# Paired first loads, first products by parts, and a LayerNorm whose sums go through fp32r products

## The chip, the cores and the metric

The kernel runs on one NeuronCore of a Trainium2 chip. A NeuronCore has five engines that run side by side, each through its own queue, in order: TensorE (PE) multiplies matrices, VectorE (DVE) works on two tensors or a tensor and a number, ScalarE (ACT) applies functions and casts, GpSimd (POOL) does simple tensor work and issues some transfers, SyncE (SP) issues most transfers. They wait for one another through semaphores. The metric is the time of one execution on the device in microseconds; less is better.

## What is computed

One layer of a decoder trunk, for 256 new positions of a prompt and 8 x 4 sampled ones, together T = 288 columns. All is float32 at the boundary.

```python
h = rmsnorm(x, norm1_g)                                    # 2048 wide
a, gate, z = split(h @ w_in + b_in, 3)                     # 1024 each
u = a * sigmoid(gate)
c = silu(layernorm(depthwise_causal_conv(u, conv_w, conv_b), ln_g, ln_b))
d = multiscale_pool(z)                                     # windows 2, 4, 8, 16
p = (d @ pool_w per group) * pool_scale
x = x + concat(c, p) @ w_out
x = x + square(relu(rmsnorm(x, norm2_g) @ w_ff1)) @ w_ff2  # 8192 wide inside
y = rmsnorm(x, norm_f)
```

The outputs are y for both groups of requests and the new states of the convolution and of the pool. The LayerNorm takes mean and variance over the 1024 channels of the convolution:

```python
mu = mean(xf); var = mean(square(xf - mu))
y = (xf - mu) * rsqrt(var + EPS) * g + b
```

## The kernel before

The activations lie transposed: channels on the 128 partitions, the 288 columns along the row. A weight block is 128x1024 (four rows of tiles of 256 columns); a product multiplies a 128x128 tile of it with 128x288 of activations into a bank of PSUM. Since the matrix unit takes fp32r, a rounded float32, for its fast products, each float is split in two, a high part (the cast) and a low part (what is left). Each 128x128x288 step is then three products: high by high, high by low and low by high. `wr` is a raw block of weights as it is loaded, `whi` its high part (cast on ACT, line 275), `wlo` its low part (a subtraction on DVE, line 280, or on POOL in halves, line 283, or a transfer that adds). Numbers behind such a name count the blocks. High and low parts have five buffers each: `whi73` goes where `whi67` was, one stage of loads earlier by the rotation, and waits until the last product that reads `whi67` has been made. All such products are made by `mm` on line 306, from `gemm`, which goes through a list of (row k, bank m, part of the weight, part of the activation).

The order of the stages is fixed by `SEQUENCE`: the input projection, by pairs of banks (c0 to c7 for the convolution, p0 to p3 for the pool), the small products of the pool groups (P0 to P3), w_out in eight pairs of banks (`ac18` to `ac21` and so on) first over the pool's half (`dx`, whose parts are made on line 510) and then over the convolution's (`mx`, line 592), then the two feed-forward products, which make up the larger part of the time. A scheduler places the instructions of each engine by a priority, which is the order in which the code is written; `later()` adds to it, so that what stands under it is put behind other ready work.

The start is special, since nothing is loaded. `first_weights` loads the rows of the first four banks, `first_x` the activations, in the order of `FIRST`: the first two rows apart, then pairs. The very first weights and the second ones are issued on ACT's queue, with a table load between them; all else on SP's. `first_split` makes high and low parts, x before weights. The first four banks are multiplied row by row (`singly=True`). The RMSNorm is applied after the products: `squares` adds the squares of x, `rsqrt_sums` (lines 242 to 257) sums them on PE in 96x3, takes the root on ACT and corrects it on DVE, and `spread` brings the 288 values to all partitions by three products with `ident`. They go into the stream of products by the table `between`.

The LayerNorm of the convolution works the same way inside the w_out stage. `ln_mean` (two fp32 products, each two passes on PE, into `pmean`) stands in the pair g = 5; `ln_sums` subtracts the mean from the four tiles c1 to c4 (line 559), squares and adds them (`q`), and sums by `rsqrt_sums` in g = 6; `ln_rows` spreads them in g = 7. Then each tile is multiplied by the row (`n`, line 587), goes through Silu twice, once for each half (line 590), and is split (`mx`, lines 592 and 593).

ACT has one table of functions loaded at a time; `load_table` runs a tiny activation (`few`, line 209) in order to load another. `inverse_root` (lines 232 to 237) is the other form of the corrected root, for a whole tile of 288 columns; it is used before the feed-forward.

Of the kernel before, what the change touches and what calls it, by code (L numbers as in the profile page):

```python
# [86 lines left out]
def trunk_kernel(ctx: ExitStack, tc: tile.TileContext, io):  # L87
# [97 lines left out]
    def first_weights(k, n, queue):  # L185
        if k % 2 == 0:
            raws.append(by_pair(raw_tile()))
        src = io["w"][1 + k // 8 : 4 + k // 8 : 2].rearrange("b p k c -> p b k c")
        queue.dma_start(raws[k // 2][:, :, k % 2 : k % 2 + n, :], src[:, :, k % 8 : k % 8 + n, :])

    def first_x(k, n):
        nc.sync.dma_start(xT[:, k : k + n, :], io["xT"][:, k : k + n, :])

    FIRST = [(0, 1), (1, 1)] + [(k, 2) for k in range(2, KT, 2)]
    first_weights(0, 1, nc.scalar)
    nc.sync.dma_start(vec[:, 0:NG], io["vec"][:, 0:NG])
    for k, n in FIRST[:6]:
        first_x(k, n)
        if k > 1:
            first_weights(k, n, nc.sync)  # L200
# [10 lines left out]
    with tc.issue_after(load_table(AF.Sqrt, ones[:, 0:1]).ins):  # L211
        first_weights(1, 1, nc.scalar)
# [14 lines left out]
    cst = const.tile([P, 32], F32, name="cst")  # L227
# [83 lines left out]
    def gemm(banks, rhs, m_outer=False, between={}, classes="", singly=False):  # L311
# [4 lines left out]
        units = [(k, 2) for k in range(0, n, 2)]  # L316
        if singly:
            units = [(k, 1) for k in range(n)]
        pairs = [(k, width, m) for k, width in units for m in range(len(banks))]
        if m_outer:  # L320
            pairs.sort(key=lambda p: p[2])
        parts = {1: ((0, 0, 0), (0, 0, 1), (0, 1, 0)), 2: ((0, 0, 0), (1, 0, 0), (0, 1, 0), (1, 1, 0), (1, 0, 1), (0, 0, 1))}
        todo, begins = [], {}
        for k, width, m in pairs:
            if m == 0:
                begins[len(todo)] = k
            todo += [(k + d, m, w, x) for d, w, x in parts[width]]
# [27 lines left out]
    def first_split(k0, n):  # L355
        for k in range(k0, k0 + n):
            if k % 2 == 0:
                hx.extend(halves(act2("hx")))
            hh, hl = hx[k]
            if k == 0:  # L360
                nc.vector.tensor_scalar(hh, xT[:, k, :], v("norm1_g", k), None, op0=ALU.mult)  # L361
            else:
                nc.scalar.activation(hh, xT[:, k, :], AF.Copy, scale=v("norm1_g", k))
# [70 lines left out]
    def conv_pair(i, banks):  # L434
# [7 lines left out]
        if i == N8 - 1:  # L442
            load_table(AF.Sqrt, tg[:, 0:1])
# [335 lines left out]
```

## Time and profile before

| | |
|---|---|
| median of 3 runs | 1085.36 us (1085.34 to 1086.2) |
| the profiled execution | 1084.97 us, span 1082.9 us |
| TensorE busy | 1071.1 us, 99%, 8198 records |
| VectorE busy | 636.5 us, 59% |
| ScalarE busy | 477.4 us, 44% |
| GpSimd busy | 173.8 us, 16% |
| first product of the layer | 5.58 us |
| first product that reads mx | 219.33 us |

The profiled execution is one of its own; a sum worked out on its trace is compared with its own time. A record of PE is one pass: an fp32 product makes two. Products overlap in the pipeline, so a record's length (about 0.29 us for 288 columns) is more than the distance between two starts (0.13 us). A row of the timeline gives the start, the length to the end of the last of the joined instructions, the engine, the line, the operation, output and inputs, how many were joined, and in brackets the idle time before and what ended it. Rows of groups by line have the least, median and longest length in ns and the first and last start.

### The profile page before, as it was taken

The numbers are of one execution on the slowest core, as the hardware profiler recorded it, in microseconds if no ns is written. First come the engines' busy times: TensorE is split into PE (matmuls) and PEld (weight loads), VectorE is DVE, ScalarE is ACT, GpSimd is POOL, SyncE is SP. The second block draws the span as 40 slices with busy tenths as digits, with TensorE's granted clock in tenths as the row PEclk, the third lists the DMA queues.
The fourth block names the chain that finished last, engine by engine and source line by source line (L and its number), as shares of the span: only waits on it lengthen the run. The fifth ranks groups of instructions, "written<-read, shape, count | busy, mean of one in ns | idle before, by whom it ended". The sixth has DMA issues, their size and how long they took to land.

```text
span 1082.9 us, 19574 instructions
## 1 busy us (share of the span) xinstructions
PE 1071.1 (99%) x8198; PEld 1068.5 (99%) x8198; DVE 636.5 (59%) x817; ACT 477.4 (44%) x584; POOL 173.8 (16%) x180
## 2 busy tenths in 40 slices
PE   9999999999999999999999999999999999999996
PEld 8999999999999999999999999999999999999996
DVE  8899999678655544445544444545544445554552
ACT  8654455475544433334443333444433334444441
POOL 0878979512000000000000000000000000000001
PEclk9999999999999999999999999999999999999998
DMA  9896477545555555555555555555555555555522
GB/s 333 281 268 182 137 209 231 172 152 176 173 163 170 174 168 165 175 164 168 175 169 165 174 167 167 174 171 164 172 169 166 173 172 164 171 172 163 172 78 88
DMA packets 58696, 190.71 MB, mean 176 GB/s; under 512 B 6256, under 2 KB 12016, under 8 KB 58608
## 3 DMA queue, kind: packets, MB, share of 16 engines
q1 hardware_dynamic: 56336, 184.09, 53.0%
q0 software_dynamic: 1008, 3.67, 1.8%
q10 hardware_dynamic: 1264, 1.70, 0.5%
q8 instruction: 64, 1.05, 0.4%
q14 instruction: 24, 0.20, 0.1%
HBM read 185.16 MB, written 4.28 MB: 175 GB/s over the span
## 4 chain that ended last, share of the span: by engine, by line
PE 76%; issue 21%; ACT 1%; DMA 1%; DVE 1%; POOL 0%; SPq 0%; POOLq 0%; DVEq 0%
PE ac L306 75%; DMA wr<-in_w 1%; PE pp L306 0%; ACT whi L275 0%; DVE wlo L280 0%; POOL xT L715 0%; ACT n L590 0%; DVE z_all L414 0%; ACT L209 0%; ACT z_all L412 0%; PE pt L306 0%; PE pmean L306 0%; POOLq L765 0%; DVE xT L690 0%; DVE n L587 0%
## 5 line engine op out<-in xcount | busy, mean ns | idle before, releaser
L275 ACT CAST whi<-wr 128x1024 fp32r<-128x1024 f32 (+1 forms) x341 | 355.5, 1043 | 557.5 <-PE ac L306 536.0
L280 DVE TENSOR_TENSOR wlo<-wr,whi 128x1024 fp32r<-128x1024 f32 (+1 forms) x297 | 363.7, 1225 | 348.4 <-ACT whi L275 348.4
L306 PE MATMUL ac<-ax,whi 128*128 128x288 f32 x2048 | 351.1, 292 | 0.0
L306 PE MATMUL ac<-fx,whi 128*128 128x288 f32 x2048 | 350.2, 292 | 0.0
L306 PEld LDWEIGHTS ac<-ax,whi 128*128 128x128 f32 x2048 | 296.0, 187 | 0.0
L306 PEld LDWEIGHTS ac<-fx,whi 128*128 128x128 f32 x2048 | 295.7, 187 | 0.0
L306 PE MATMUL ac<-ax,wlo 128*128 128x288 f32 x1024 | 217.4, 292 | 0.0
L306 PE MATMUL ac<-fx,wlo 128*128 128x288 f32 x1024 | 216.4, 292 | 0.0
L306 PEld LDWEIGHTS ac<-ax,wlo 128*128 128x128 f32 x1024 | 162.6, 187 | 0.0
L306 PEld LDWEIGHTS ac<-fx,wlo 128*128 128x128 f32 x1024 | 162.3, 187 | 0.0
L306 PE MATMUL ac<-hx,whi 128*128 128x288 f32 x768 | 136.2, 293 | 0.7 <-DVE hx L361 0.3
L715 POOL TENSOR_TENSOR xT<-xT,rf 128x288 f32<-128x288 f32 x4 | 3.0, 792 | 800.1 <-ACT rf L719 800.1
L306 PEld LDWEIGHTS ac<-hx,whi 128*128 128x128 f32 x768 | 113.3, 188 | 1.4 <-ACT whi L275 0.9
L283 POOL TENSOR_TENSOR wlo<-wr,whi 128x512 fp32r<-128x512 f32 x74 | 100.6, 1415 | 35.4 <-ACT whi L275 34.4
L457 DVE SCALAR_TENSOR_TENSOR pc<-u_all,vec,pc 128x256 f32<-128x256 f32 x232 | 99.5, 483 | 1.9 <-ACT pc L454 0.7
L306 PE MATMUL ac<-hx,wlo 128*128 128x288 f32 x384 | 86.2, 293 | 0.3 <-DVE wlo L280 0.2
L306 PEld LDWEIGHTS ac<-hx,wlo 128*128 128x128 f32 x384 | 62.7, 188 | 0.7 <-DVE wlo L280 0.7
L306 PE MATMUL ac<-dx,whi 128*128 128x288 f32 x256 | 46.1, 296 | 0.3 <-ACT dx L510 0.3
L306 PE MATMUL ac<-mx,whi 128*128 128x288 f32 x256 | 45.2, 294 | 0.1
L659 DVE SCALAR_TENSOR_TENSOR t<-ac,r 128x576 f32<-128x576 f32 x32 | 24.2, 758 | 25.2 <-PE ac L306 25.2
L306 PEld LDWEIGHTS ac<-dx,whi 128*128 128x128 f32 x256 | 37.9, 188 | 0.7 <-ACT dx L510 0.6
L306 PEld LDWEIGHTS ac<-mx,whi 128*128 128x128 f32 x256 | 37.5, 188 | 0.6 <-ACT mx L592 0.3
(130 smaller groups left out, 515.0 us busy)
## 6 DMA issues: line engine op xcount, KB each, us to landing
wr<-in_w SPq DMA_DIRECT2D x335, 512.0 KB, 3.7
wlo<-in_w POOLq DMA_DIRECT2D x7, 512.0 KB, 8.5
xT<-in_xT SPq DMA_DIRECT2D x7, 288.0 KB, 7.1
out_u_out<-u_all SPq DMA_DIRECT2D x1, 1208.0 KB, 8.9
u_all<-in_hist_c SPq DMA_DIRECT2D x8, 136.0 KB, 5.6
wr<-in_w SPq DMA_DIRECT2D x4, 256.0 KB, 3.5
out_z_out<-z_all SPq DMA_DIRECT2D x1, 668.0 KB, 8.9
z_all<-in_hist_p SPq DMA_DIRECT2D x4, 152.0 KB, 7.7
```

What stands on the lines that cost most here:

```text
L275: nc.scalar.copy(hi, raw)
L280: nc.vector.tensor_tensor(lo, raw, f32(hi), op=ALU.subtract)
L283: nc.gpsimd.tensor_tensor(lo[:, j : j + 2, :], raw[:, j : j + 2, :], f32(hi[:, j : j + 2, :]), op=ALU.subtract)
L306: last = nc.tensor.matmul(*args, **kw)
L457: nc.vector.scalar_tensor_tensor(out=dst, in0=up[:, w : w + SEQ], scalar=cwv[:, w : w + 1], in1=pc, op0=ALU.mult, op1=ALU.add)
L659: nc.vector.scalar_tensor_tensor(out=t, in0=bk[:, :, :T], scalar=0.0, in1=both(rows2[0]), op0=ALU.max, op1=ALU.mult)
L715: eng.tensor_tensor(xk, xk, r[:, None, :].to_broadcast([P, n, T]), op=ALU.mult)
```

## The change

Six things are changed together.

1. *First loads.* x and weights are loaded in pairs of rows throughout. The first weights come as two transfers, one for each block of two banks, with both rows of the pair; the first on ACT's queue, the second on SP's behind the joint x of rows 0 and 1. ACT's queue issues one transfer at the start, not two.
2. *First split.* The high cast of a weight comes ahead of the x parts, and the low part of a weight ahead of the low parts of x. The first two pairs are cast in two halves, by blocks of banks.
3. *First products.* For the first four banks, `by_part` lists all high by high products of a pair of rows, then all with the low weights, then all with the low x; the first pair does so for two banks and then for the other two. The table `classes`, which sets the alternation of two kinds of products, now covers the start.
4. *Table load.* The table with Sqrt is loaded after the last `dx` of the pool and not after the last sigmoid.
5. *LayerNorm.* The two inputs of the mean are split into fp32r parts (`hm`: two casts on ACT, a subtraction on POOL and one on DVE), and the mean is four fp32r products with `means_c`, a copy of `ones` (1/1024 everywhere) in fp32r, made by POOL at the start. The sum of squares is split likewise (`hs`), two fp32r products bring the sums to all partitions at once (`pt`), so that `spread` is not needed; the root is taken of the whole 128x288, and `inverse_root` corrects it (reciprocal and three steps on 128x288 in place of 96x3).
6. *Priority.* From the subtraction of the mean to the split of `mx`, all stands under `later(-LATER)`, that is ahead of other work.

```diff
-    def first_weights(k, n, queue):
...
+    def first_weights(k, queue, blocks):
         src = io["w"][1 + k // 8 : 4 + k // 8 : 2].rearrange("b p k c -> p b k c")
+        queue.dma_start(raws[k // 2][:, blocks], src[:, blocks, k % 8 : k % 8 + 2, :])
+
+    def first_load(k):
+        raws.append(by_pair(raw_tile()))
+        nc.sync.dma_start(xT[:, k : k + 2, :], io["xT"][:, k : k + 2, :])
+        if k:
+            first_weights(k, nc.sync, slice(0, 2))
+        else:
+            first_weights(k, nc.scalar, slice(0, 1))
+            first_weights(k, nc.sync, slice(1, 2))
...
-    with tc.issue_after(load_table(AF.Sqrt, ones[:, 0:1]).ins):
-        first_weights(1, 1, nc.scalar)
+    load_table(AF.Sqrt, ones[:, 0:1])
...
+        if by_part:
+            for k in range(0, n, 2):
+                sets = [range(len(banks))] if k else [range(2), range(2, len(banks))]
+                for last, ms_ in enumerate(sets, 1 - len(sets)):
+                    for part, (w, x) in enumerate(((0, 0), (1, 0), (0, 1))):
...
+                        todo += [(k + (1 - d if x else d), m, w, x) for m in ms_ for d in range(2)]
...
-        if i == N8 - 1:
-            load_table(AF.Sqrt, tg[:, 0:1])
...
-    chain.append(gemm(pair0 + pair1, hx, between={15: first_sums}, singly=True))
-    third = conv_products(2, between={2: first_rows}, classes="01" * 18 + TURN)
+    chain.append(gemm(pair0 + pair1, hx, between={15: first_sums}, classes="01" * 18 + TURN, by_part=True))
+    third = conv_products(2, between={2: first_rows}, classes="01" * 9 + TURN)
...
+    load_table(AF.Sqrt, f32(mixp[1][0])[:, 0:1])
...
+    hm = actp.tile([P, 4, T], F32R, name="hm", tag="act")
+    for (hi, lo), part, eng in (((1, 0), sum_c[:, 0, :], nc.gpsimd), ((3, 2), cs[-1][:, 1, :], nc.vector)):
+        nc.scalar.copy(hm[:, hi, :], part)
+        eng.tensor_tensor(hm[:, lo, :], part, f32(hm[:, hi, :]), op=ALU.subtract)
...
-        mm(norm["mean"], ones, sum_c[:, 0, :], start=True, stop=False)
-        return mm(norm["mean"], ones, cs[-1][:, 1, :], start=False, stop=True)
+        return products(norm["mean"], [hm[:, j, :] for j in (1, 0, 3, 2)])
...
-        norm["sums"] = rsqrt_sums([ssc[:, 0, :]], 1.0 / DC, AF.Silu)
...
+            nc.scalar.copy(hi, ssc[:, 0, :])
+            nc.vector.tensor_tensor(lo, ssc[:, 0, :], f32(hi), op=ALU.subtract)
+            bk, rl = ms("pt"), row("rl")
+            mean, root = bk[:, 0, :T], bk[:, 1, :T]
+            last = products(mean, [hi, lo])
+            nc.scalar.activation(root, mean, AF.Sqrt, bias=eps)
+            load_table(AF.Silu, root[:, 0:1])
+            inverse_root(mean, root, rl, root)
...
-    BETWEEN = {5: {4: ln_mean}, 6: {6: ln_sums}, 7: {2: ln_rows}}
+    BETWEEN = {5: {4: ln_mean}, 6: {6: ln_sums}}
...
+        with later(-LATER):
+            n = tmpp.tile([P, 2, T], F32, name=nm("n"), tag="ag", bufs=2)
...
```

The scheduler moves the instructions of the engines with it. At the start this is DVE's queue before; `hx1` holds both parts of the first two rows of x, `wlo1` the low part of the first weights:

```order
L361 TENSOR_SCALAR hx1_162<-xT_86,vec_85 128x288 [waits DMAHW2_49,DMAHW1_49]
L280 TENSOR_TENSOR wlo1_166<-wr1_92,whi1_165 128x2x256 [waits DMAHW0_49,Activation_49]
L364 SCALAR_TENSOR_TENSOR hx1_162<-xT_86,vec_85,hx1_162 128x288 [waits DVE_49]
L280 TENSOR_TENSOR wlo1_166<-wr1_92,whi1_165 128x2x256 [waits DMAHW3_49,Activation_49]
L364 SCALAR_TENSOR_TENSOR hx1_162<-xT_86,vec_85,hx1_162 128x288 [waits DMAHW4_49,Activation_49]
L364 SCALAR_TENSOR_TENSOR hx2_173<-xT_86,vec_85,hx2_173 128x288 [waits DMAHW5_49,Activation_49]
```

And now:

```order
L375 TENSOR_TENSOR wlo1_167<-wr1_93,whi1_166 128x512 [waits DMAHW0_49,Activation_49]
L369 TENSOR_SCALAR hx1_168<-xT_86,vec_85 128x288 [waits DMAHW2_49,DMAHW1_49]
L378 SCALAR_TENSOR_TENSOR hx1_168<-xT_86,vec_85,hx1_168 128x288 [waits Activation_49]
L378 SCALAR_TENSOR_TENSOR hx1_168<-xT_86,vec_85,hx1_168 128x288 [waits DVE_49]
L375 TENSOR_TENSOR wlo1_167<-wr1_93,whi1_166 128x512 [waits DMAHW3_49,Activation_49]
L378 SCALAR_TENSOR_TENSOR hx2_179<-xT_86,vec_85,hx2_179 128x288 [waits DMAHW4_49,Activation_49]
```

The first work on DVE was the high part of x, row 0; it now stands behind a low part of weights, which waits for the first cast.

At the end of the LayerNorm, ACT's queue before, from the root of the sums (st2, 96x3) on; n1 and n2 are the first two tiles that go through Silu:

```order
L251 ACTIVATE st2_2708<-st2_2708 96x3 [waits DVE_49]
L209 ACT_TABLE_LOAD
L209 ACTIVATE few_111<-st2_2708 96x1 [waits Activation_49]
L275 CAST whi71_2890<-wr71_2886 128x1024 [waits DMAHW0_49,PE_49]
L590 ACTIVATE n1_2808<-n1_2808,vec_85 128x288 [waits DVE_49]
L590 ACTIVATE n1_2808<-n1_2808,vec_85 128x288
L275 CAST whi72_2894<-wr72_2888 128x1024 [waits DMAHW1_49,PE_49,Pool_49]
L590 ACTIVATE n2_2815<-n2_2815,vec_85 128x288 [waits DVE_49]
L590 ACTIVATE n2_2815<-n2_2815,vec_85 128x288
L592 CAST mx1_2812<-n1_2808 128x576 [waits Activation_49]
L592 CAST mx2_2819<-n2_2815 128x576 [waits Activation_49]
L275 CAST whi73_2961<-wr73_2957 128x1024 [waits DMAHW2_49,PE_49]
```

And now, from the cast of hs:

```order
L586 CAST hs_2714<-q21_2699 128x288 [waits DVE_49]
L591 ACTIVATE pt2_2717<-pt2_2717,cst_163 128x288 [waits PE_49]
L209 ACT_TABLE_LOAD
L209 ACTIVATE few_114<-pt2_2717 128x1 [waits Activation_49]
L276 CAST whi71_2898<-wr71_2894 128x1024 [waits DMAHW7_49,PE_49]
L276 CAST whi72_2902<-wr72_2896 128x1024 [waits DMAHW0_49,PE_49,Pool_49]
L276 CAST whi73_2969<-wr73_2965 128x1024 [waits DMAHW1_49,PE_49]
L614 ACTIVATE n1_2816<-n1_2816,vec_85 128x288 [waits DVE_49]
L614 ACTIVATE n1_2816<-n1_2816,vec_85 128x288
L614 ACTIVATE n2_2823<-n2_2823,vec_85 128x288 [waits DVE_49]
L614 ACTIVATE n2_2823<-n2_2823,vec_85 128x288
L616 CAST mx1_2820<-n1_2816 128x576 [waits Activation_49]
```

The cast whi73 has moved from behind both mx to ahead of the first Silu; the root is now on 128x288 and waits for PE.

On PE in that place now, the last products of ac21, which read whi67, and the first that read mx:

```order
L307 MATMUL ac21_2754<-dx4_2043,wlo67_2744 128x288 x2
L307 MATMUL ac21_2754<-dx4_2043,whi67_2743 128x288 x4
L307 MATMUL ac21_2754<-dx4_2043,wlo67_2744 128x288 x2
L307 MATMUL ac21_2754<-dx4_2043,whi67_2743 128x288 x2
L307 MATMUL ac22_2845<-mx1_2820,whi69_2807 128x288 [waits DVE_49,Activation_49]
L307 MATMUL ac22_2845<-mx1_2820,whi69_2807 128x288
```

The pair of spreading products that stood in ac21 is gone; that the first product with mx1 follows directly on the last with whi67 is as before.

DVE around the sums before:

```order
L566 TENSOR_TENSOR q21_2689<-q21_2689 128x288 [waits DVE_49]
L280 TENSOR_TENSOR wlo70_2804<-wr70_2797,whi70_2803 128x1024 [waits DMAHW7_49,Activation_49]
L250 TENSOR_SCALAR st2_2708<-pt2_2704 96x3 [waits PE_49]
L254 RECIPROCAL st2_2708<-st2_2708 96x3 [waits Activation_49]
L255 TENSOR_TENSOR st2_2708<-st2_2708 96x3 [waits DVE_49]
L256 SCALAR_TENSOR_TENSOR st2_2708<-st2_2708 96x3 [waits DVE_49]
L257 SCALAR_TENSOR_TENSOR st2_2708<-st2_2708 96x3 [waits DVE_49]
L582 TENSOR_TENSOR xT_86<-xT_86,ac20_2651 128x576 [waits PE_49]
L280 TENSOR_TENSOR wlo71_2891<-wr71_2886,whi71_2890 128x1024 [waits DMAHW0_49,Activation_49]
L587 TENSOR_TENSOR n1_2808<-c1_637,pt2_2704 128x576 [waits PE_49]
```

And now:

```order
L583 TENSOR_TENSOR q21_2699<-q21_2699 128x288 [waits DVE_49]
L281 TENSOR_TENSOR wlo70_2812<-wr70_2805,whi70_2811 128x1024 [waits DMAHW6_49,Activation_49]
L587 TENSOR_TENSOR hs_2714<-q21_2699,hs_2714 128x288 [waits Activation_49]
L235 RECIPROCAL rl1_2718<-pt2_2717 128x288 [waits Activation_49]
L605 TENSOR_TENSOR xT_86<-xT_86,ac20_2661 128x576 [waits PE_49]
L281 TENSOR_TENSOR wlo71_2899<-wr71_2894,whi71_2898 128x1024 [waits DMAHW7_49,Activation_49]
L236 SCALAR_TENSOR_TENSOR pt2_2717<-pt2_2717,rl1_2718 128x288 [waits DVE_49]
L237 SCALAR_TENSOR_TENSOR pt2_2717<-pt2_2717,rl1_2718 128x288 [waits DVE_49]
L238 SCALAR_TENSOR_TENSOR pt2_2717<-pt2_2717,rl1_2718 128x288 [waits DVE_49]
L281 TENSOR_TENSOR wlo72_2903<-wr72_2896,whi72_2902 128x1024 [waits DMAHW0_49,Activation_49]
L611 TENSOR_TENSOR n1_2816<-c1_640,pt2_2717 128x576 [waits DVE_49]
```

The low part of hs stands behind wlo70, and between the reciprocal and n1 there are now an addition to xT, two weights' low parts and three steps on 128x288.

More of the change, by code (lines that the diff above doesn't have):

```diff
@@ L549, in trunk_kernel, with products @@
     norm = {}
+    hm = actp.tile([P, 4, T], F32R, name="hm", tag="act")
+    for (hi, lo), part, eng in (((1, 0), sum_c[:, 0, :], nc.gpsimd), ((3, 2), cs[-1][:, 1, :], nc.vector)):
+        nc.scalar.copy(hm[:, hi, :], part)
+        eng.tensor_tensor(hm[:, lo, :], part, f32(hm[:, hi, :]), op=ALU.subtract)
+    def products(bank, parts):
+        for j, part in enumerate(parts):
+            last = mm(bank, means_c, part, start=j == 0, stop=j == len(parts) - 1)
+        return last
     def ln_mean():
```

120 lines of the change are left out of this document (57 added, 63 removed).

## Prediction

> **What bounds the kernel now.** I read the page first, then busy time by stretches, then the timeline of TensorE (PE) at the three places that the change touches, and there the timelines of the engines that PE waits for.
>
> The page's shares and the stretches (us, PE busy, PEld, DVE, ACT, POOL, clock, DMA share, GB/s):
>
> ```profile
> PE 1071.1 (99%) x8198; PEld 1068.5 (99%) x8198; DVE 636.5 (59%) x817; ACT 477.4 (44%) x584; POOL 173.8 (16%) x180
> 5.58:34.99 29.41, 28.75 (x211) 27.68 (x211) 27.45 (x40) 25.14 (x42) 6.69 (x5) 1.00 1.02 369
> 240.00:1073.00 833.00, 832.79 (x6412) 832.59 (x6411) 420.39 (x408) 339.17 (x386) 11.33 (x12) 1.00 0.51 163
> ```
>
> PE is the bound. From 240 us on 6412 products fill 833.00 us, 129.9 ns each, and nothing is to be had there: the change leaves their number alone. So it must be judged by what PE loses or wins before 240 us. From 5.58 to 34.99 us 211 records take 29.41 us, 2.0 more than at 129.9 ns: that is all that the head could give. What PE starts at those places, as start, length, kind and count:
>
> ```profile
> 5.58 0.66 PE L306 MATMUL ac<-hx,whi 128*128 128x288 f32 x3 [0.33 <-DVE hx L361]
> 6.52 0.40 PE L306 MATMUL ac<-hx,whi 128*128 128x288 f32 x1 [0.27 <-DVE hx L364]
> ...
> 17.62 0.40 PE L306 MATMUL ac<-hx,wlo 128*128 128x288 f32 x1
> ...
> 34.99 0.91 PE L306 MATMUL pt<-ident,st 96*128 96x96 f32 x6
> ...
> 170.16 0.43 PE L306 MATMUL ac<-dx,whi 128*128 128x288 f32 x2
> 170.94 0.66 PE L306 MATMUL ac<-dx,whi 128*128 128x288 f32 x3 [0.34 <-ACT dx L510]
> ...
> 200.94 0.65 PE L306 MATMUL pmean<-sum_c,ones 128*128 128x288 f32 x2
> ...
> 202.18 0.30 PE L306 MATMUL ac<-dx,wlo 128*128 128x288 f32 x1
> ...
> 209.91 0.59 PE L306 MATMUL pt<-ones,q 128*96 128x1 f32 x6
> ...
> 210.71 0.42 PE L306 MATMUL ac<-dx,wlo 128*128 128x288 f32 x2
> ...
> 213.62 0.80 PE L306 MATMUL pt<-ident,st 96*128 96x96 f32 x6
> ...
> 214.56 0.29 PE L306 MATMUL ac<-dx,wlo 128*128 128x288 f32 x1
> ...
> 218.80 0.43 PE L306 MATMUL ac<-dx,whi 128*128 128x288 f32 x2
> 219.33 0.53 PE L306 MATMUL ac<-mx,whi 128*128 128x288 f32 x2
> 219.70 0.43 PE L306 MATMUL ac<-mx,wlo 128*128 128x288 f32 x2
> ```
>
> In a group the starts lie 0.13 apart; after a pause the second product comes about 0.1 late as well (219.33 to 219.70 for two products is 0.37, not 0.26). I call that 0.1 a restart.
>
> **Head.** The first product will come later: DVE's first work is now a low half of weights, which wants the first cast and its block, ahead of the x that used to be first:
>
> ```profile
> 4.60 0.62 ACT L275 CAST whi<-wr 128x512 fp32r<-128x512 f32 x1 [1.88 <-DMA wr<-in_w]
> 5.35 0.68 DVE L280 TENSOR_TENSOR wlo<-wr,whi 128x512 fp32r<-128x512 f32 x1
> ```
>
> That is 4.60 + 0.62 + 0.68 = 5.90 and then the x part, shorter than the low part: the first product near 6.3 instead of 5.58. In return the pause before 6.52 and others like it go, since high by high products of several banks come before a low half is wanted. At 17.62 PE waits for the fifth low half either way; there it is two products further on, 0.26 us. That lead meets a gate. The sums of RMSNorm go to PE now four products later, and the products that spread the result (34.99) keep their place; what leads to them is:
>
> ```profile
> 31.05 1.05 ACT L275 CAST whi<-wr 128x1024 fp32r<-128x1024 f32 x1 [1.99 <-DMA wr<-in_w]
> 32.54 0.94 DVE L255 TENSOR_TENSOR st<-st 96x3 f32<-96x3 f32 x1
> 33.52 1.22 DVE L256 SCALAR_TENSOR_TENSOR st<-st 96x3 f32<-96x3 f32 x1
> 32.18 2.54 POOL L283 TENSOR_TENSOR wlo<-wr,whi 128x512 fp32r<-128x512 f32 x2 [0.45 <-ACT whi L275]
> ```
>
> The root starts at 32.10, behind a cast which waited for a transfer, and two tiny DVE operations end (33.48 and 34.74) as POOL's two halves do (each 1.27 of the 2.54: 33.45 and 34.72); 0.16 or so later PE has its operand. Nothing in that chain is shortened, except as the transfers land earlier. So most of the lead is waited away at 34.99. Bounds: the chain comes 0.2 us later, because the sums do (+0.3), or the joint transfers carry the whole queue forward and the gate moves with the cast, which had 1.99 us idle before it; with the lead and as much again that PE's first waits leave, about a third of the 2.0 (-0.7). I take -0.15, near the chain that does not move. The x casts and the low parts of this stage stand in other places on ACT and DVE, but as often.
>
> **Table load.** Before, it stands between a sigmoid and the cast that PE wants at 170.94:
>
> ```profile
> 169.00 1.28 ACT L209 ACT_TABLE_LOAD   x1
> 170.29 0.20 ACT L209 ACTIVATE few<-tg 128x1 f32<-128x1 f32 x1
> 170.40 0.48 ACT L510 ACTIVATE dx<-pp,vec 128x288 fp32r<-128x288 f32 x1
> 174.59 1.05 ACT L275 CAST whi<-wr 128x1024 fp32r<-128x1024 f32 x1 [1.88 <-POOL prd L460]
> 169.92 0.63 DVE L445 SCALAR_TENSOR_TENSOR u_all<-ac,vec,tg 128x256 f32<-128x256 f32 x2
> ```
>
> PE's step from the second product at 170.16 (170.29) to 170.94 is 0.65, so 0.52 is lost, and 0.1 for the restart. With the load gone the cast is ready 1.4 us earlier. The next thing that is late is the bank which the two u_all operations read until 170.55: PE can go on at about 170.6, and loses the restart still. Gain 0.3 to 0.6; I take -0.45. After the last dx the load falls into the 1.88 us in which ACT idles before 174.59, and costs nothing there. Without that idle time it would cost its 1.28 us plus 0.20 on a cast of weights, which PE wants later.
>
> **LayerNorm, what PE saves.** The mean takes from 200.94 to 202.18 with two ordinary products in it: 1.24 - 0.26 = 0.98. Four fp32r products take 4 x 0.13 = 0.52. Gain 0.45. The sums take from 209.91 to 210.71 with two ordinary ones: 0.54; two products take 0.26. Gain 0.28. The spreading of rows takes from 213.62 to 214.56 with two ordinary ones, 0.94 - 0.26 = 0.68, and goes altogether: 0.70 with the late record before it. Together -1.4. The casts that make the mean's parts (two on ACT, one each on POOL and DVE) work on tensors for which PE does not wait at 200.94, and are hidden behind products; were that cover gone they would cost at most about a POOL half, 1.3 us.
>
> **LayerNorm, what PE waits for.** Two new waits, both from the order of the queues. The rows they are made of:
>
> ```profile
> 197.56 0.68 PE L306 MATMUL ac<-dx,whi 128*128 128x288 f32 x4
> 198.02 1.05 ACT L275 CAST whi<-wr 128x1024 fp32r<-128x1024 f32 x1 [1.94 <-PE ac L306]
> 208.74 0.46 DVE L566 TENSOR_TENSOR q<-q 128x288 f32<-128x288 f32 x1
> 209.64 1.23 DVE L280 TENSOR_TENSOR wlo<-wr,whi 128x1024 fp32r<-128x1024 f32 x1 [0.44 <-ACT whi L275]
> 216.63 1.03 ACT L275 CAST whi<-wr 128x1024 fp32r<-128x1024 f32 x1
> 217.57 1.15 ACT L590 ACTIVATE n<-n,vec 128x288 f32<-128x288 f32 x2
> 218.62 1.23 ACT L592 CAST mx<-n 128x576 fp32r<-128x576 f32 x2
> L643 ACT ACTIVATE mean<-mean,cst x1: 476/476/476, 285.2 to 285.2; 128x288 f32<-128x288 f32 x1
> L234 DVE RECIPROCAL r<-mean x1: 1958/1958/1958, 285.7 to 285.7; 128x288 f32<-128x288 f32 x1
> 219.27 0.76 DVE L582 TENSOR_TENSOR xT<-xT,ac 128x576 f32<-128x576 f32 x1 [0.34 <-PE ac L306]
> ```
>
> First, hs. Its low part stands on DVE behind wlo70, which wants whi70, which wants the buffer that the last product of whi66 frees; the two products of hs come 14 places after that product, 14 x 0.13 = 1.82 us. A cast starts 0.33 after the start of the product that frees its buffer (198.02 against the second of the four at 197.56). Chain: 0.33 + 1.05 + 1.23 + 0.04 + 0.46 = 3.1. PE waits 1.3, and restarts: +1.4. It could be 1.0 without the restart, if the overlaps of DVE's neighbours (some 0.08 each) count. Queued behind on PE is all the rest of ac20.
>
> Second, mx1. On ACT whi73 now stands ahead of both silu pairs and of mx1's cast. It reuses the buffer of whi67, whose last reader is the last product of ac21, and the very next product on PE wants mx1. So PE cannot have work while ACT does whi73, four silus and the cast, however early the LayerNorm is done. By the row times: 0.33, then from a weight cast through one pair and mx1 to PE 219.33 - 216.63 = 2.70, and a second pair 218.62 - 217.57 = 1.05: 4.08 from start to start, 3.95 lost, 4.05 with the restart. This is the floor. The other chain runs from the late hs product: 0.35 to the root (0.48), load 1.28, few 0.20, the reciprocal on a whole tile 1.96 (it was 96x3), xT 0.75, wlo71 1.23, three steps on 128x288 at 0.5 (as at 208.74), wlo72 1.23, n1 0.75 (as xT): some 9.5 us, against 60 products (7.8) and 0.33 + 1.05 until whi73 is done, 9.2. They end together; the later of them makes the pause 4.0 to 4.5, and I take 4.2. Before, the same place lost 0.53 - 0.13 = 0.40, 0.1, and another 0.23 behind it: 0.73, which goes. So +3.5. Behind mx1 the second bank, mx2 and the casts of later weights are then all ready; the queue of transfers has only waited.
>
> LayerNorm: -1.4 + 1.4 + 3.5 = +3.5.
>
> **Sum.** -0.15 - 0.45 + 3.5 = +2.9. The profiled execution took 1084.97 us (span 1082.9 and 2.1 around it), 0.39 below the median of 1085.36; 1084.97 + 2.9 = 1087.9 for such an execution, and on the median 1088.2.
>
> **Rivals.** *It ends within the noise.* About 0.2%, 2.2 us, is what can be told from no change here, so below 1087.5 it counts as none. If the head keeps its 0.7, the table load gives 0.6, the second pause is at its floor (4.05 less 0.73) and hs at 1.1 with its restart, the sum is -0.7 - 0.6 - 1.4 + 1.1 + 3.3 = +1.7: 1087.1. For it speaks that the DMA engines are full (1.02) until 34.99, so that better transfers would count; against it the gate at 34.99.
>
> *Not slower.* The second wait isn't there: mx1 is cast before PE gets to it, as in 218.62 to 219.33. That needs whi73 to find its buffer free some 4 us before the last product of ac21 ends, or the cast to pass it. From there, -0.15 - 0.45 - 1.4 + 1.4 - 0.7 = -1.3: 1084.0; with hs on time as well, 1082.6, faster. The order of ACT speaks against it.
>
> *Slow products after the pause.* PE has no pause above 0.75 us in this trace after its start, but it starts slowly:
>
> ```profile
> 1.04 4.21 PE L215 MATMUL warm<-ones 128*128 128x128 f32 x18 [1.04 <-DVE cst L230]
> ```
>
> Eighteen records take 213 ns for 128 columns, 1.7 ns each, where the mean's four of 288 take 0.24 us, 0.84 ns each: half speed for 4 us, though the granted clock reads 1.00. If a pause of 4 us brings that state back, another 4 us of work runs at half speed and loses 2: 1090.2. The Trainium skill, "TensorE: Matmul & The Clock Gate", Part 1 on the clock gate, states such a rule: half clock after an idle window of about 3.4 us, in windows that run freely, and full clock after a busy one. By that rule an estimate is that a pause of 4.1 us holds a whole window in one run of five, and then costs 1.7 to 3.4.
>
> **Chances.** My forecast, 1087.5 to 1089.0: 0.55. Slow products: 0.13. Within the noise by small sums: 0.20. Without the second pause: 0.09, of which 0.05 is faster. What is left, 0.03, I give to a larger pause. So slower 0.71, same 0.24, faster 0.05. The range runs from 1086.8, a little under the small sum, to 1090.3, the slow products; it leaves the cases without the second pause out, and some of the larger pause.
>
> **What would show it.** In the changed profile: the first product near 6.3 and the spread products at 34.7 to 35.1; no pause at 170.3 above 0.3; PE waiting for DVE hs about 1.3 us near 210; then ac<-mx starting 4 us after the last ac<-dx, with ACT's row "whi, n x4, mx" filling it; and a step of 130 ns behind it, or 260 if the last rival holds. I am wrong if ACT begins whi73 well before that last product, or if the products after 223 us stay behind for another reason, such as weights that arrive late.

## The result, and the profile after

The changed kernel takes 1091.02 us (median of 6 executions, 1090.82 to 1097.71) against 1085.35 (1085.2 to 1086.2): ratio 1.007, 95% interval 1.0054 to 1.0086. It is slower, by 5.7 us, where 2.9 were forecast, and outside the forecast's range (1086.8 to 1090.3). The executions of this kernel fall in two groups, one at 1090 to 1091 and one at 1096 to 1098, with one at 1093 between; the profiled one took 1096.03 us and is of the second, so its trace holds some 5 us that the median does not.

The page of the changed kernel, its busy times and the stretches in which the clock falls (us, PE busy, PEld, DVE, ACT, POOL, clock, DMA share, GB/s):

```profile
PE 1073.5 (98%) x8188; PEld 1070.6 (98%) x8188; DVE 647.1 (59%) x819; ACT 480.4 (44%) x588; POOL 174.5 (16%) x182
204.00:206.00 2.00, 0.00 (x0) 0.00 (x0) 2.00 (x1) 0.00 (x0) 2.00 (x2) 1.00 0.60 199
208.00:210.00 2.00, 2.00 (x10) 2.00 (x10) 2.00 (x5) 1.87 (x3) 0.00 (x0) 0.50 0.45 162
232.00:234.00 2.00, 2.00 (x10) 2.00 (x10) 0.70 (x2) 1.87 (x4) 0.00 (x0) 0.50 0.32 129
```

PE is idle for two whole microseconds at 204, which it never was before, and behind each long pause ten records of PE fall into two microseconds, where stretches at full clock have 16 or 17; the granted clock there is 0.50.

PE's timeline after, at the places that were quoted of before:

```profile
6.68 0.77 PE L307 MATMUL ac<-hx,whi 128*128 128x288 f32 x4 [1.43 <-DVE hx L369]
...
35.94 0.91 PE L307 MATMUL pt<-ident,st 96*128 96x96 f32 x6
...
79.84 0.53 PE L307 MATMUL ac<-hx,wlo 128*128 128x288 f32 x2 [0.33 <-DMA wlo<-in_w]
...
202.22 0.55 PE L307 MATMUL pmean<-hm,means_c 128*128 128x288 f32 x3
206.66 0.60 PE L307 MATMUL pmean<-hm,means_c 128*128 128x288 f32 x1 [3.88 <-DVE hm L560]
207.06 0.68 PE L307 MATMUL ac<-dx,whi 128*128 128x288 f32 x2
...
217.78 0.40 PE L307 MATMUL pt<-hs,means_c 128*128 128x288 f32 x1 [0.90 <-DVE hs L587]
...
225.74 0.43 PE L307 MATMUL ac<-dx,whi 128*128 128x288 f32 x2
229.96 0.53 PE L307 MATMUL ac<-mx,whi 128*128 128x288 f32 x2 [3.79 <-ACT mx L616]
```

Two of the three long pauses are those of the prediction (hs and mx), near the forecast size. The first, 3.88 us for `hm`, is not in it. What it waits for, on DVE, beside POOL's row (its operations back to back) and ACT:

```profile
197.86 8.75 DVE L560 TENSOR_TENSOR hm<-c,hm 128x288 fp32r<-128x288 f32 x1 [0.50 <-ACT hm L559]
...
198.80 7.50 POOL L284 TENSOR_TENSOR wlo<-wr,whi 128x512 fp32r<-128x512 f32 x6
...
202.56 1.05 ACT L276 CAST whi<-wr 128x1024 fp32r<-128x1024 f32 x1 [2.20 <-PE pmean L307]
```

A subtraction of 288 columns, which takes 0.46 us elsewhere, takes 8.75 and ends (206.61) when POOL's row of six halves ends (206.30).

The same main product (the n-th behind the first, of 8112 that write `ac` or `pp`) in both traces, after less before, shows where the time arose in that execution:

| main product | before, us | shift, us | what lies since the row above |
|---|---|---|---|
| first | 5.58 | +1.10 | later first product |
| 384th | 59.33 | +0.88 | start |
| 1152nd | 159.27 | +1.76 | the wait for a transfer at 79.84 |
| 1400th | 192.62 | +1.28 | table load: -0.47 |
| 1476th | 203.51 | +6.44 | mean: pause 4.05, slow products 1.5, saving 0.45 |
| 1530th | 211.23 | +7.58 | sums: pause 1.3, saving 0.2 to 0.3 |
| 1580th | 218.54 | +6.94 | spreading gone: -0.65 |
| 1610th | 223.24 | +11.79 | pause ahead of mx 3.35 net, slow products 1.5 |
| 8100th | 1067.62 | +11.73 | nothing |

### The profile page after: what moved, and what is told of

The parts are those of the page before. It is cut to its first block, busy times and chain, and to the rows that moved or that the text cites. A ratio compares the mean times of both kernels' runs of the same rounds, so it can differ in the third digit from the quotient of the medians.

```text
span 1094.3 us, 19556 instructions
## 1 busy us (share of the span) xinstructions
PE 1073.5 (98%) x8188; PEld 1070.6 (98%) x8188; DVE 647.1 (59%) x819; ACT 480.4 (44%) x588; POOL 174.5 (16%) x182
## 3 DMA queue, kind: packets, MB, share of 16 engines
q8 instruction: 64, 1.05, 0.4%
## 4 chain that ended last, share of the span: by engine, by line
PE 74%; issue 20%; DVE 2%; DMA 2%; ACT 1%; POOL 0%; SPq 0%; POOLq 0%; DVEq 0%
PE ac L307 74%; DMA wlo<-in_w 1%; DVE hm L560 1%; DMA wr<-in_w 1%; PE pp L307 1%; DVE pc L463 0%; POOL xT L739 0%; ACT whi L276 0%; ACT n L614 0%; PE pt L307 0%; ACT hx L371 0%; ACT whi L366 0%; DVE z_all L422 0%; ACT z_all L420 0%; DVE wlo L375 0%
## 5 line engine op out<-in xcount | busy, mean ns | idle before, releaser
L276 ACT CAST whi<-wr 128x1024 fp32r<-128x1024 f32 (+1 forms) x332 | 348.0, 1049 | 559.8 <-PE ac L307 535.6
L281 DVE TENSOR_TENSOR wlo<-wr,whi 128x1024 fp32r<-128x1024 f32 x288 | 353.6, 1228 | 346.0 <-ACT whi L276 346.0
L307 PE MATMUL ac<-hx,whi 128*128 128x288 f32 x768 | 131.3, 294 | 1.6 <-DVE hx L369 1.4
L307 PE MATMUL ac<-hx,wlo 128*128 128x288 f32 x384 | 80.1, 294 | 0.6 <-DMA wlo<-in_w 0.3
L307 PEld LDWEIGHTS ac<-hx,wlo 128*128 128x128 f32 x384 | 60.5, 188 | 1.1 <-DMA wlo<-in_w 0.6
```

Source lines behind the costliest of these rows:

```text
L276: nc.scalar.copy(hi, raw)
L281: nc.vector.tensor_tensor(lo, raw, f32(hi), op=ALU.subtract)
L307: last = nc.tensor.matmul(*args, **kw)
```

## The experiments

The theories: A, the wait for `hm` is in every execution and makes the difference to the forecast; B, it is long in the second group only, and the rest of the difference is the clock behind the pauses. Later C (the granted clock of PE falls behind a pause) and D (what holds DVE) by themselves.

**The changed kernel again.**

> The changed kernel as it is. In its profiled execution (1096.03 us, 5 us above the median) DVE's low part of the mean's second input took 8.75 us beside POOL's halves and PE waited 3.9 us for it. Theory A: that wait is in every execution, so a profiled one at 1091 shows a row of 6 to 9 us too and the 5 us lie elsewhere. Rival B: the wait is in the slow executions only; one at 1091 shows the low part in under 1 us and no wait of PE at the mean, and its 5.7 us over the kernel before are the pause ahead of mx (4.1), hs (1.3), slow products behind the pause (1.5) and a later start (0.9 and 0.9), less the savings.

Four executions, 1089.92 to 1097.98, median 1094.79; the profiled one took 1096.51 and has the same row again (8.73 us, PE idle 3.87). Of the ten executions of this kernel four lie at 1096 to 1098, and the median of all ten is 1092.1. All three profiled executions of kernels with this LayerNorm fell in the second group, so neither theory could be read off here. No execution near 1091 has a trace.

**Both low parts of the mean on POOL.**

```diff
-    for (hi, lo), part, eng in (((1, 0), sum_c[:, 0, :], nc.gpsimd), ((3, 2), cs[-1][:, 1, :], nc.vector)):
+    for (hi, lo), part, eng in (((1, 0), sum_c[:, 0, :], nc.gpsimd), ((3, 2), cs[-1][:, 1, :], nc.gpsimd)):
```

> One edit: the low part of the mean's second input is made on POOL, not DVE, in the row of POOL's own halves. Theory A (every execution has the wait): 4.0 to 5.5 us less, 1085.5 to 1087. Rival B (only the slow ones have it): the median stays at 1090.5 to 1091.2 and executions of 1096 and more are gone. Both: no pause of PE at the mean above 0.3 us.

1090.21 us (1089.36 to 1092.16, 4 executions): no execution above 1092.2, the median 0.8 lower, no pause at the mean. That is 0.3 under the range that B gave and 3.2 above A's, so A is out. But POOL's row is one operation longer now, and an addition of squares on DVE, behind it, took 2.11 us; PE waited twice for hs, 1.16 and 0.64 us. In the trace the clock fell behind the pause ahead of mx here as well.

**The LayerNorm as before, and the start as before.** The first keeps the changed start and the moved table load, the second the table load and the LayerNorm.

The first, against the changed kernel:

```diff
-        return products(norm["mean"], [hm[:, j, :] for j in (1, 0, 3, 2)])
+        mm(norm["mean"], ones, sum_c[:, 0, :], start=True, stop=False)
+        return mm(norm["mean"], ones, cs[-1][:, 1, :], start=False, stop=True)
...
-            last = products(mean, [hi, lo])
...
-            inverse_root(mean, root, rl, root)
+        norm["sums"] = rsqrt_sums([ssc[:, 0, :]], 1.0 / DC, AF.Silu)
...
+    BETWEEN = {5: {4: ln_mean}, 6: {6: ln_sums}, 7: {2: ln_rows}}
```

> The LayerNorm as before, with the changed start and the moved table load. From the shifts between the two traces (start +0.9, a wait for an accumulating transfer at 79 us +0.9, table load -0.45): 1086.7. If the start's loss is particular to that execution: 1084.9. My forecast on record had -0.6 for the two: 1084.8.

1085.01 us (1084.37 to 1085.63, 10 executions) against 1085.14: ratio 0.9998 (0.9989 to 1.0007), no change that can be told. In its trace the first product comes at 6.63, the shift behind the start is +1.05, and the table load then takes 0.49 off; the wait at 79 us is not there.

The second, against the changed kernel:

```diff
-    def first_load(k):
...
+    FIRST = [(0, 1), (1, 1)] + [(k, 2) for k in range(2, KT, 2)]
+    first_weights(0, 1, nc.scalar)
...
-    chain.append(gemm(pair0 + pair1, hx, between={15: first_sums}, classes="01" * 18 + TURN, by_part=True))
+    chain.append(gemm(pair0 + pair1, hx, between={15: first_sums}, singly=True))
```

> The start as before, with the moved table load and the changed LayerNorm. If start and LayerNorm add up: 1091.0 less 1.8 = 1089.2. If the wait for the accumulating transfer comes from the new start only in some executions: 1090. The pauses at the mean, at hs and ahead of mx should stand as in the changed kernel.

1090.65 us (1090.43 to 1096.89, 5 executions), both groups again, and above both values that were expected. So the LayerNorm alone makes the loss; the start adds little, and not the 1.8 of that one trace.

**The mean alone.** The kernel before with the fp32r mean, the low part on DVE.

```diff
+    for (hi, lo), part, eng in (((1, 0), sum_c[:, 0, :], nc.gpsimd), ((3, 2), cs[-1][:, 1, :], nc.vector)):
+        nc.scalar.copy(hm[:, hi, :], part)
+        eng.tensor_tensor(hm[:, lo, :], part, f32(hm[:, hi, :]), op=ALU.subtract)
...
-        mm(norm["mean"], ones, sum_c[:, 0, :], start=True, stop=False)
-        return mm(norm["mean"], ones, cs[-1][:, 1, :], start=False, stop=True)
+        return products(norm["mean"], [hm[:, j, :] for j in (1, 0, 3, 2)])
```

> The kernel before with one part of the change: the mean by fp32r products, DVE making the low part of its second input; sums, spreading, table load and start as before. Theory B2 (DVE's low part is held back by POOL's halves in some executions and not in others): two sets of times, 1084.6 (the 0.5 that the products save) and about 1090 (a wait of 4 and slow products of 1.5 to 2.3). Theory A2 (held back in every execution): all near 1090. If the changed LayerNorm around it is what delays DVE: all near 1084.6. The profile should show the row of the low part at 8.7 us where PE waits.

1085.62 us (1084.98 to 1087.34, 11 executions), ratio 1.0004 (0.9995 to 1.0013): neither of the two groups that were expected. The trace shows why, DVE and POOL of this run:

```profile
196.96 5.79 DVE L555 TENSOR_TENSOR hm<-c,hm 128x288 fp32r<-128x288 f32 x1 [0.50 <-ACT hm L554]
...
197.40 5.04 POOL L285 TENSOR_TENSOR wlo<-wr,whi 128x512 fp32r<-128x512 f32 x4
202.78 2.56 POOL L285 TENSOR_TENSOR wlo<-wr,whi 128x512 fp32r<-128x512 f32 x2 [0.34 <-ACT whi L277]
```

In these traces DVE's subtraction is held for as long as POOL's row is unbroken. Here the row had a gap of 0.34 us at 202.44, since POOL waited for a cast, and DVE ended in it (202.75). PE then waited 0.92 us, which eats the saving of the mean. In the changed kernel's trace the cast (202.56 to 203.61) was done before POOL was through with the fourth half (198.80 + 4 x 1.25 = 203.80), so there was no gap, and DVE was held for two more halves. What makes one execution of the changed kernel have the gap and another not was not traced.

**The mean and the table load, both low parts on POOL.** Start, sums and spreading as before.

```diff
-        if i == N8 - 1:
-            load_table(AF.Sqrt, tg[:, 0:1])
...
+    load_table(AF.Sqrt, f32(mixp[1][0])[:, 0:1])
...
+    for (hi, lo), part, eng in (((1, 0), sum_c[:, 0, :], nc.gpsimd), ((3, 2), cs[-1][:, 1, :], nc.gpsimd)):
...
+        return products(norm["mean"], [hm[:, j, :] for j in (1, 0, 3, 2)])
```

> The kernel before with the moved table load and the mean by fp32r products, both low parts on POOL; sums, spreading and start as before. Table load -0.45, mean -0.45 to -0.55, no pause at the mean, the pause ahead of mx at its old 0.4: 1084.1 to 1084.4, in one set of times. If the second POOL part comes late or holds a low part of weights: 1085 or more, with a pause of PE near 200.

1085.01 us, ratio 0.9996 (0.9987 to 1.0005): the time of the unfavourable branch, but not by its reason, since PE does not pause near 200. The rows are DVE's and PE's:

```profile
203.99 2.11 DVE L575 TENSOR_TENSOR q<-q,q 128x576 f32<-128x576 f32 x1
...
209.88 0.64 PE L308 MATMUL pt<-ones,q 128*96 128x1 f32 x6 [0.61 <-DVE q L576]
```

Up to the mean it was 0.80 ahead. Then POOL's row, longer by the moved subtraction, held an addition of squares on DVE for 2.11 us (0.75 elsewhere), until that row ended, and PE waited for the sums. It looks like the same hold, on a later operation.

**26 products in the pause ahead of mx**, with both low parts on POOL.

```diff
+    with tc.issue_after(last):
+        for j in range(26):
+            nc.tensor.matmul(fill, means_c, mixp[0][0], start=j == 0, stop=j == 25)
```

> The changed kernel with both low parts of the mean on POOL, and 26 products into a bank that nobody reads between the last product of ac21 and the first with mx1. They add no result. Theory C (the pause closes the clock gate and the products behind it run at half speed): the wait for mx1 stays, its idle part falls from 3.8 to about 0.4, no step of 0.240 us follows, the granted clock stays 1.00, and the time is 1.5 to 2.3 less than with the low parts on POOL alone (1090.2), 1088 to 1088.7, within 0.5 between executions. If the steps of 0.240 come from something else (late weights): no change, 1090.2.

1089.42 us (1089.04 to 1089.6), 0.8 less than without, where 1.5 to 2.3 were expected. Behind the pause ahead of mx there is no slow product any more, but in the trace there are some behind the waits for hs, which the other run's trace does not have. PE, then the clock:

```profile
210.20 0.40 PE L307 MATMUL pt<-hs,means_c 128*128 128x288 f32 x1 [1.16 <-ACT hs L586]
211.24 0.41 PE L307 MATMUL pt<-hs,means_c 128*128 128x288 f32 x1 [0.64 <-DVE hs L587]
...
212.00:214.00 2.00, 2.00 (x12) 2.00 (x11) 0.32 (x1) 1.72 (x4) 0.00 (x0) 0.59 0.65 205
216.00:218.00 2.00, 2.00 (x17) 2.00 (x16) 1.97 (x4) 0.00 (x0) 0.00 (x0) 1.00 0.00 0
```

So two idle stretches of 1.16 and 0.64 us with a product between can halve the clock as well. They did here and not in the trace without the 26 products, which has the same two. The record of the granted clock accounts for it. Within the layer its half-speed stretches are 3.41 us long, or twice that, and where a trace has two of them they begin a whole number of 3.41 us apart (206.69 and 230.59 in the changed kernel's, seven times), so the clock is set anew on a grid of 3.41 us. On that grid both idle stretches fall into one piece here; without the 26 products a boundary at 209.70 parts them. This run, then the one without (length of the piece, then PE's busy time; the clock stands third from the end):

```profile
208.95:212.36 3.41, 1.61 (x10) 1.31 (x10) 2.20 (x4) 1.09 (x3) 0.00 (x0) 1.00 0.62 168
212.36:215.77 3.41, 3.41 (x16) 3.41 (x15) 2.09 (x2) 2.32 (x3) 0.00 (x0) 0.50 0.43 139
...
206.29:209.70 3.41, 2.50 (x20) 2.27 (x18) 3.38 (x6) 1.52 (x3) 0.00 (x0) 1.00 0.52 157
209.70:213.11 3.41, 2.52 (x17) 2.31 (x18) 1.24 (x2) 1.86 (x3) 0.00 (x0) 1.00 0.72 222
213.11:216.53 3.42, 3.42 (x27) 3.42 (x27) 3.11 (x3) 1.48 (x4) 0.00 (x0) 1.00 0.18 72
```

A piece in which PE is idle for 1.80 of 3.41 us is followed by one at half speed; pieces with 0.91 and 0.89 idle are not. These slow products do not account for the missing part of the saving, though: the other three executions took 1089.0 to 1089.5 at mean granted clocks of 0.997 and 0.998, which are those of the kernel before. What does is open.

**DVE's second operand in PSUM.** The changed kernel, with the high part copied to PSUM by ACT.

```diff
-        eng.tensor_tensor(hm[:, lo, :], part, f32(hm[:, hi, :]), op=ALU.subtract)
+        high = f32(hm[:, hi, :])
+        if eng is nc.vector:
+            nc.scalar.copy(pm[:, 1, :T], high)
+            high = pm[:, 1, :T]
+        eng.tensor_tensor(hm[:, lo, :], part, high, op=ALU.subtract)
```

> The changed kernel with one edit: ACT copies the high part of the mean's second input to PSUM as well, and DVE subtracts that copy, so that its low part reads one tensor from SBUF and one from PSUM. Theory D (DVE stands still because both of its inputs come from SBUF while POOL's halves run): the low part takes 0.45 to 0.6 us, PE does not pause at the mean, and the two sets of times (1090 to 1091 and 1096 to 1098) become one near 1089 to 1090.5. If DVE is held back for another reason (its place in the queue, the output in fp32r): 6 to 9 us as before, two sets.

1089.86 us (1089.32 to 1090.46, 4 executions), one group. DVE, POOL and then PE of this run:

```profile
197.48 0.46 DVE L565 TENSOR_TENSOR hm<-c,pmean 128x288 fp32r<-128x288 f32 x1 [0.94 <-ACT pmean L563]
...
197.91 7.64 POOL L284 TENSOR_TENSOR wlo<-wr,whi 128x512 fp32r<-128x512 f32 x6
...
223.52 0.85 PE L307 MATMUL ac<-mx,whi 128*128 128x288 f32 x2 [3.78 <-ACT mx L621]
224.16 0.68 PE L307 MATMUL ac<-mx,wlo 128*128 128x288 f32 x2
```

The same subtraction, at the same place in the row and with the same fp32r output, takes 0.46 us, and POOL's row is as before. Only where the second input lies was changed: D is confirmed, and the three later runs with the copy have 0.46 as well. The median is 1.16 lower than that of the changed kernel's first six executions, about the loss of a hold that ends in a gap (in the run with the mean alone PE's step there was 1.22 instead of 0.13). No execution near 1096 is left, here or in the 13 of the next two runs.

**The same with the 26 products.**

> As the first of these runs, with the 26 products that add no result in the pause ahead of mx1. Theory C (the clock gate): 1.5 to 2.3 less than that run, 1088 to 1088.6, with no step of 0.240 us; that would be my forecast's own sum (1088.2) with the gate and the held-up low part taken out. If the gate is not it: the same time as that run.

1087.92 us (1087.3 to 1088.88, 7 executions), 1.94 less, though these products add nothing to the result. PE and the clock:

```profile
219.31 3.63 PE L630 MATMUL fill<-dx,means_c 128*128 128x288 f32 x26
223.27 0.53 PE L307 MATMUL ac<-mx,whi 128*128 128x288 f32 x2 [0.33 <-ACT mx L621]
223.64 0.42 PE L307 MATMUL ac<-mx,wlo 128*128 128x288 f32 x2
...
224.00:226.00 2.00, 2.00 (x17) 2.00 (x16) 2.00 (x4) 0.56 (x2) 0.00 (x0) 1.00 0.71 227
```

The first product with mx1 is as late as before; the third product comes 0.37 after it, not 0.64, and the clock stays at 1.00. C is confirmed. In the two traces the place itself (1580th to 1610th main product) costs 4.77 us without these products and 3.33 with them, 1.4 less; the rest of the 1.94 lies within the spread of the executions. What is left, 1087.92, is the kernel of the forecast's sum.

**whi73 behind mx on ACT**, on top of that.

```diff
-        nc.scalar.copy(hi, raw)
+        with tc.issue_after(hold[0]) if hold else nullcontext():
+            nc.scalar.copy(hi, raw)
...
+            hold.append(first_mx[1])
```

> As the run with 26 products, with one more edit: the cast whi73 is put behind both casts of mx on ACT. By my forecast both chains, ACT's row and the LayerNorm's own, end together, so the wait for mx1 falls by 0.1 to 0.3 only, and the time with it. If whi73's place alone makes the pause: 1.0 less (its length). If DVE's low part of whi73, which now comes later, holds up the low parts of mx: slower by up to 1.

1088.34 us (1087.76 to 1088.8), not faster; in the traces PE's idle time ahead of mx1, behind the 26 products, falls from 0.33 to 0.30 us:

```profile
223.71 0.53 PE L308 MATMUL ac<-mx,whi 128*128 128x288 f32 x2 [0.30 <-ACT mx L622]
```

So the cast's place isn't what makes the pause by itself; the chain of the LayerNorm takes as long, as the forecast had it: ACT now waits 3.00 us for DVE's `n`, and begins the first Silu 1.24 us after the last product of ac21 starts, where it was 1.28.

**The parts that save, without those that wait.** The kernel before with the moved table load and the fp32r mean, its low part against the copy in PSUM; sums, spreading and start as before.

```diff
-    for (hi, lo), part, eng in (((1, 0), sum_c[:, 0, :], nc.gpsimd), ((3, 2), cs[-1][:, 1, :], nc.gpsimd)):
+    for (hi, lo), part, eng in (((1, 0), sum_c[:, 0, :], nc.gpsimd), ((3, 2), cs[-1][:, 1, :], nc.vector)):
...
+            nc.scalar.copy(pm[:, 1, :T], high)
+            high = pm[:, 1, :T]
```

The diff is against the kernel with both low parts on POOL and the table load.

> The kernel before with the moved table load and the mean by fp32r products, its second low part by DVE against the copy in PSUM; sums, spreading and start as before. POOL's row is as short as before, so the additions of squares behind the mean should not be held up as they were with both low parts on POOL (2.11 us for one of them). Expected -0.45 and -0.45: 1084.4 to 1084.6; 1085.0 if the additions are held up all the same.

1084.25 us (1083.74 to 1084.73, 11 executions) against 1085.26: ratio 0.9990 (0.9982 to 0.9999). It is the fastest kernel here: 1.0 us under the kernel before, 0.8 under the next, though the upper end of the interval is close to 1. PE at the mean and ahead of mx:

```profile
200.92 0.69 PE L308 MATMUL pmean<-hm,means_c 128*128 128x288 f32 x4
201.44 0.43 PE L308 MATMUL ac<-dx,whi 128*128 128x288 f32 x2
...
218.46 0.43 PE L308 MATMUL ac<-dx,whi 128*128 128x288 f32 x2
218.96 0.53 PE L308 MATMUL ac<-mx,whi 128*128 128x288 f32 x2
```

Four products at 0.13 with no pause, and mx where it was: its step is 0.37. The first addition of squares is still held, for 1.40 us, but PE does not wait for it as it did with both low parts on POOL.

## Why the prediction was wrong, and where it was right

The direction was right, the size was half. Two terms are missing from the sum: the hold of DVE's low part of `hm`, which it put at nothing, and the slow products, which it kept as a rival. With the slow products alone the forecast's own figure was 1090.2, inside its range; the hold takes the time out of it. By its own steps:

- *Head, -0.15.* Wrong by some 0.4, as far as can be told. The first product came at 6.47 to 6.77 in the traces with the new start, not 6.3, and the shift behind the start was -0.2 to +1.1 us (0 to +0.45 in the four with the old start). Start and table load together gave -0.1 (1085.01 against 1085.14, with an interval of about 1 us either way), the table load alone takes 0.47 in the traces, so the start costs about 0.3. The lead of two products that the step counted on was there in one of the eight traces.
- *Table load, -0.45.* Right: the shift falls by 0.47 in the changed kernel's trace, and by 0.43 to 0.49 in every other that has the edit.
- *What PE saves in the LayerNorm, -1.4.* Right: 0.45 to 0.5 at the mean where nothing else disturbs it (the last run), 0.65 at the spreading.
- *"Hidden behind products; were that cover gone they would cost at most about a POOL half, 1.3 us."* This step failed. It took the longest hold to be one half of POOL's, as in the row that the prediction quotes (two DVE operations on 96x3, 0.94 and 1.22 us, that ended as POOL's halves did), and so put the term at nothing. The subtraction was held to the end of POOL's row instead, 8.75 us, where the cover was about 4.8 (it began at 197.86, and PE wanted its result near 202.6): PE stood 3.88 us. Where the row has no gap, mean and sums cost 5.6 to 6.6 us more than in the run with the copy in PSUM and the 26 products, by the three traces, slow products behind the pause included. In the median of the changed kernel's first six executions the hold costs 1.16.
- *hs, +1.4.* Right in size: in the traces without the hold the stretch with the sums costs 1.2 net, so 1.5 with the saving of 0.28 that the forecast counts apart. It comes as two waits there, 0.46 us for the cast and 0.64 for the low part, and not as the one for the low part. In the changed kernel's trace PE's step is 1.30.
- *The pause ahead of mx, +4.2.* Right: 4.08 from the start of the last product to the first with mx1, the forecast's floor (4.08); that ACT's row and the LayerNorm's chain end together is borne out by the run that moved whi73.
- *Slow products after the pause*, a rival with 0.13 and +2.0. This step failed too, since the case came true in every trace whose pause was left empty. It costs 1.94 by the medians of two runs that differ in the 26 products, and by the traces at that place 1.4 to 1.5 where the half speed lasts 3.41 us and 2.3 where it lasts 6.83. The estimate of one run in five asked for a pause that holds a whole window; the traces show that 1.80 us of idle time in one are enough, and a pause of 3.8 us leaves at least 1.9 in one of those that it touches. The 1.00 that the prediction read beside the slow warm-up products is no reading: the trace before has no record of the clock until 5.64 us.

The sum without the two missing terms was 1088.2; the kernel with neither (the low part against PSUM, the pause filled) takes 1087.92. That they agree so closely is in part luck: in that run's trace the head is +0.66 and not -0.15 and the pause ahead of mx +3.33 and not +3.5, and 0.6 comes back behind the last main product. The steps from 1087.92 to 1089.86 and to 1091.02 are differences of medians, so they say what the two terms cost and check nothing further. That the executions near 1091 have a short hold is inferred: from the run with the mean alone, and from their mean granted clock of 0.995, since the traced executions with one stretch of 3.41 us at half speed have 0.995 and 0.996, and those with more of it 0.991 to 0.994. None of them was traced.

## What to carry to other kernels

Before a vector operation is counted as hidden, look at what GpSimd does in that stretch and where both operands lie: with both in SBUF it may get no turn until GpSimd's row breaks, however short it is, and one operand in PSUM set it free here. A pause of PE near 4 us is to be charged with another 1.4 to 2.3 us for half-speed products, and here it was better to let PE multiply something useless than to let it stand. A chain of few long instructions that replaces many short ones on a small tile (a reciprocal on 288 columns for one on 3) is to be compared by the time to its end, not by the instructions that the busiest engine saves.

## What the runs showed of the hardware

- *A DVE operation with both inputs in SBUF can wait for a gap in POOL's row.* The subtraction took 8.73 to 8.75 us beside six and more halves in three traces, 5.79 where the row broke, and 0.46 in the four traces with one input in PSUM. The Trainium skill, "SBUF — State Buffer", sections "SBUF: two separate sides" and "Who interferes with whom", states the rule: such an operation and a GpSimd operation that reads SBUF take a shared pair of ports as an exclusive lock, one whole instruction at a time. The trace agrees on which operands are concerned, PSUM included. It differs on how long: in the three traces DVE was not let in at seven boundaries between GpSimd's instructions, and ended 0.32 us after the last of them. This is not always so: in the trace before, the first of the two operations on 96x3 ended at 33.48, where one half of POOL's ends (33.47) and the next follows without a gap. What decides who is next is open.
- *PE's clock falls to half behind a pause of 3.8 to 3.9 us.* In all eight such pauses that were traced without the 26 products (two each in three traces with the long hold, one each in the runs with both low parts on POOL and with PSUM) there were steps of 0.240 us instead of 0.130, at a granted clock of 0.50 for 3.41 us (four of them) or 6.83 us (four, begun inside the pause). Behind the three that were filled there were none. Between 100 and 240 us, each 3.41 us piece at full clock with 1.80 to 3.41 us of idle time was followed by half speed, nine in all, and none with 1.09 or less was. The Trainium skill, "TensorE: Matmul & The Clock Gate", Part 1, gives an idle window of about 3.4 us that runs freely. The length and the free running agree with the traces. By that rule an estimate is that a pause of 3.8 us holds a whole one in about one case of nine. The runs show that less than a wholly idle window is enough.
- *At the start*, in two of the eight traces with the new start (first product at 6.77 and 6.68 us) the clock fell to 0.50 for 3.41 us, from 8.29 and 7.43 on, though PE had run the warm-up products until 5.13 and 4.72: idle for 1.64 and 1.96 us between. In two others 1.59 and 1.69 us between did not do it. In two more traces, one of them with the old start, products stand 0.24 us apart until 9.5, where the record of the clock begins. The shift that is left behind the start in the first two, +0.9 and +0.6, is within what the others show, since PE waits for other things there.
